# A two-layer decoder trunk on one core: the second layer's input scaled before its split, and places chosen by an assignment

## The chip, the cores and the metric

The kernel runs on one core of one Trainium2 chip, in one launch. The metric is the device time of an execution, in microseconds. Before the change the median of three runs was 2044.93 us (2044.12 to 2046.39).

## The reference

Two layers, each with an input projection that feeds four token mixers, an output projection, and a feed-forward part. All is float32, 1024 tokens by 1024 channels.

```python
for l in range(DEPTH):
    h = rmsnorm(x, attn_norm[l])
    proj = h @ w_in[l]
    (c_q, c_kv, k_r, g_b, g_c, u_conv, u_pool, q_sw, k_sw, v_sw) = jnp.split(proj, pts, axis=-1)
    y_a = mla_attention(c_q, c_kv, k_r, ...)      # latent attention, 4 heads, causal
    y_b = short_gated_conv(g_b, g_c, u_conv, ...) # width 3
    y_c = multiscale_pool(u_pool, ...)            # trailing means over 2, 4, 8, 16
    y_d = swa_sink_attention(q_sw, k_sw, v_sw, ...)  # window 128, sinks
    groups = jnp.stack([y_a, y_b, y_c, y_d], axis=2)  # each normed over its group
    x = x + mixed @ w_o[l]
    h2 = rmsnorm(x, ffn_norm[l])
    gate, up = jnp.split(h2 @ w_gate_up[l], 2, axis=-1)
    x = x + (jax.nn.silu(gate) * up) @ w_down[l]
return rmsnorm(x, final_norm)
```

`rmsnorm(x, g)` is x times the reciprocal root of its mean square ("the root" below) times a gain.

## The kernel before

Activations lie transposed: 128 channels on the partitions, tokens along a row, in tiles of 128x512. There are eight channel blocks d (or k) and two token halves t. Every float32 operand of a product is split in two: a high half in the matmul's own format (a cast on ScalarE, ACT) and a low half, the rest (a subtraction on VectorE, DVE). A product of two such operands is three matmuls, hi·hi, hi·lo, lo·hi (`mm3`, line 281 of the profile). So every weight tile and every activation costs one ACT and one DVE instruction before TensorE (PE) may use it. The feed-forward products are computed block by block with a seven-product scheme, whose sums of weight blocks POOL makes.

The norm ahead of the input projection is not applied to the input. The input x, times its gain, is split at once into `hh[k][t]`. Sums of squares are collected by `SumSq`, and `rnorm` makes the root with a matmul against ones, three ACT operations and two DVE ones; the root of a half stays in `ratt[t]`. Each projection's result in a PSUM bank is multiplied by it as it is taken out (`mul_to(f, p, r_of(t))`, the DVE rows of line 380). At the border of the layers, `done(d, t)` splits a block of the second layer's input as soon as its last down-projection has been added (`evac`, line 1723).

Tiles of SBUF come from 47 pairs of slots (`Slots`, names u), short-lived temporaries from `tmp` (te, tn, tp), results of matmuls from eight PSUM banks (names ps_). All of this is only a first draft of the program. A planner in the same file (`Order`) then traces it, gives each instruction a cost, and looks for an order of the instructions on each engine: a list schedule, then trials that shift ranks and keep what lowers the planned end, averaged over four draws of late loads. It also hands out banks and slots from the planned times, and the program is traced a second time with the order imposed. So what stands where on an engine is the planner's choice, and two programs that differ a little can be ordered quite differently.

PE's main loads in time, from the profile: the first layer's attention part (0 to about 450 us), its feed-forward part (to about 1025), the second layer's attention part (to about 1450), and its feed-forward part with the last norm (to the end).

## Time and profile before

| | before |
|---|---|
| median of three runs | 2044.93 us |
| the profiled execution | 2045.38 us |
| its span, first to last instruction | 2043.6 us |
| PE busy | 2022.9 us, 9398 records |
| DVE busy | 1578.5 us |
| ACT busy | 998.8 us |
| POOL busy | 438.9 us |
| mean granted clock of PE | 0.997 |

In the profile's rows a line number is followed by the engine, the operation, out<-in by the program's names, and the number of instructions. A row of the timeline begins with the start and the duration; what stands in brackets is the idle time of the engine before it and what released it. A line can be that of a helper: line 281 is every three-matmul product, 301 and 304 the high and the low half of a split, 223 and 224 those of a weight tile. PE's ends are modelled, so that a wait shorter than the pipeline's depth does not show as idle.

### The profile page before, as it was taken

The numbers are of one execution on the slowest core, as the hardware profiler recorded it, in microseconds if no ns is written. First come the engines' busy times: TensorE is split into PE (matmuls) and PEld (weight loads), VectorE is DVE, ScalarE is ACT, GpSimd is POOL, SyncE is SP. The second block draws the span as 40 slices with busy tenths as digits, with TensorE's granted clock in tenths as the row PEclk, the third lists the DMA queues.
The fourth block names the chain that finished last, engine by engine and source line by source line (L and its number), as shares of the span: only waits on it lengthen the run. The fifth ranks groups of instructions, "written<-read, shape, count | busy, mean of one in ns | idle before, by whom it ended". The sixth has DMA issues, their size and how long they took to land. (4 is left out here: it accounts for less than half of the span.)

```text
span 2043.6 us, 26485 instructions
## 1 busy us (share of the span) xinstructions
PE 2022.9 (99%) x9398; PEld 1672.6 (82%) x9398; DVE 1578.5 (77%) x2553; ACT 998.8 (49%) x1753; POOL 438.9 (21%) x340
## 2 busy tenths in 40 slices
PE   9999999999999999999999999999999999999998
PEld 7888788878888888888888878888788888888887
DVE  8989979998677777655657999799977777776555
ACT  7458657743333334444434576577433333354342
POOL 0300000025565661000003000000356556500000
PEclk9999999999999999999999999999999999999999
DMA  6310223435555556766513112243455555487542
GB/s 244 127 44 21 84 63 110 149 128 179 179 177 183 176 188 246 259 211 222 176 38 128 56 27 78 65 134 119 145 191 186 177 173 191 169 296 235 195 161 98
DMA packets 144133, 308.13 MB, mean 151 GB/s; under 512 B 14080, under 2 KB 61184, under 8 KB 144000
## 3 DMA queue, kind: packets, MB, share of 16 engines
q1 hardware_dynamic: 144000, 306.43, 44.4%
q8 instruction: 74, 1.21, 0.2%
q14 instruction: 59, 0.48, 0.1%
HBM read 215.67 MB, written 89.65 MB: 149 GB/s over the span
## 5 line engine op out<-in xcount | busy, mean ns | idle before, releaser
L281 PE MATMUL ps_mm<-u,u 128*128 128x512 f32 (+1 forms) x3374 | 843.5, 390 | 7.0 <-ACT u L301 2.8
L281 PEld LDWEIGHTS ps_mm<-u,u 128*128 128x128 f32 x3374 | 615.4, 189 | 129.7 <-ACT u L301 3.6
L281 PE MATMUL ps_s<-u,u 128*128 128x512 f32 x2724 | 652.0, 389 | 0.2 <-DVE u L1214 0.2
L281 PEld LDWEIGHTS ps_s<-u,u 128*128 128x128 f32 x2724 | 510.9, 188 | 108.1 <-DVE u L1214 0.6
L301 ACT CAST u<-u 128x1024 fp32r<-128x1024 f32 (+2 forms) x426 | 361.8, 868 | 478.0 <-PE ps_s L281 116.3
L304 DVE TENSOR_TENSOR u<-u,u 128x1024 fp32r<-128x1024 f32 (+2 forms) x426 | 461.3, 1100 | 154.7 <-ACT u L301 107.0
L281 PE MATMUL ps_t<-u,u 128*128 128x512 f32 (+1 forms) x1092 | 251.9, 377 | 0.0
L281 PEld LDWEIGHTS ps_t<-u,u 128*128 128x128 f32 x1092 | 196.1, 188 | 39.1 <-DVE te L380 0.5
L281 PE MATMUL ps_pv<-u,u 128*128 128x512 f32 x696 | 167.4, 389 | 0.0
L281 PEld LDWEIGHTS ps_pv<-u,u 128*128 128x128 f32 x696 | 130.6, 188 | 27.3 <-DVE tp L1670 0.3
L1277 POOL TENSOR_TENSOR u<-u 128x512 f32<-128x512 f32 x38 | 73.3, 1928 | 226.9 <-DVE u L304 174.2
L1459 ACT ACTIVATE tp<-tp 128x512 f32<-128x512 f32 x76 | 48.0, 632 | 129.3 <-DVE tp L380 129.3
L1062 POOL MEMSET u<- 128x128 f32 x32 | 6.0, 214 | 471.9 <-PE ps_mm L281 250.9
L1247 POOL TENSOR_TENSOR u<-u,u 128x512 f32<-128x512 f32 x38 | 55.6, 1464 | 205.5 <-PE ps_s L281 109.2
L770 POOL TENSOR_TENSOR u<-u,u 128x512 f32<-128x512 f32 x6 | 8.0, 1337 | 413.1 <-ACT sm L628 326.4
L301 ACT CAST u<-ps_t 128x512 fp32r<-128x512 f32 (+3 forms) x132 | 64.8, 502 | 41.3 <-PE ps_t L643 16.6
L1539 POOL TENSOR_TENSOR u<-u 128x352 f32<-128x352 f32 x64 | 79.5, 1244 | 22.4 <-DMA u<-in_w_dn 18.7
L304 DVE TENSOR_TENSOR u<-ps_t,u 128x512 fp32r<-128x512 f32 (+3 forms) x132 | 75.2, 580 | 11.4 <-ACT u L301 10.7
L306 ACT ACTIVATE u<-u,par 128x512 fp32r<-128x512 f32 x92 | 64.6, 719 | 30.7 <-DVE u L380 10.3
L1461 DVE TENSOR_TENSOR tp<-tp,u 128x512 f32<-128x512 f32 x76 | 66.4, 873 | 16.3 <-ACT tp L1459 16.2
L345 ACT ACTIVATE tn<-u 128x512 f32<-128x512 f32 (+1 forms) x91 | 52.6, 597 | 52.2 <-DVE u L1723 45.4
L1249 POOL TENSOR_TENSOR u<-u,u 128x512 f32<-128x512 f32 x38 | 71.8, 1890 | 1.6
(199 smaller groups left out, 2383.5 us busy)
## 6 DMA issues: line engine op xcount, KB each, us to landing
u<-in_w_gu SPq DMA_DIRECT2D x94, 512.0 KB, 4.0
ad<-u SPq DMA_DIRECT2D x154, 256.0 KB, 2.1
u<-ad SPq DMA_DIRECT2D x70, 512.0 KB, 6.0
u<-in_w_dn SPq DMA_DIRECT2D x64, 352.0 KB, 3.3
qd<-u SPq DMA_DIRECT2D x64, 352.0 KB, 2.8
u<-qd SPq DMA_DIRECT2D x32, 512.0 KB, 5.2
u<-in_w_in SPq DMA_DIRECT2D x28, 512.0 KB, 3.9
u<-in_w_dn SPq DMA_DIRECT2D x24, 512.0 KB, 6.5
```

The source lines that it names most:

```text
L281: pe.matmul(o, w, r, start=start and k == 0 and i == 0, stop=stop and k == n - 1 and i == 2, skip_group_check=again,)
L301: a = act.copy(hi, f)
L304: dve.tensor_tensor(out=lo, in0=f, in1=rd(hi), op=ALU.subtract)
L306: a = act.activation(hi, f, AF.Copy, scale=gain)
L345: act.activation(q, f, AF.Square)
L770: pool.tensor_tensor(out=F.ap(q + 1), in0=a21, in1=a22, op=ALU.add)
L1247: pool.tensor_tensor(out=F.ap(q + 1), in0=a21, in1=a22, op=ALU.add)
L1249: pool.tensor_tensor(out=a21, in0=F.ap(q + 1), in1=a11, op=ALU.add)
L1277: pool.tensor_tensor(out=q4, in0=q4, in1=F.ap(self.raw[1] + 1), op=ALU.add)
L1459: last_silu = act.activation(g, g, AF.Silu)
L1461: dve.tensor_tensor(out=g, in0=g, in1=r, op=ALU.mult)
L1539: pool.tensor_tensor(out=o, in0=a, in1=b, op=ALU.add)
```

## The change

Three things are changed.

1. In the second layer, the input is multiplied by gain and root first and split then (`normed`). The projections' results are therefore taken from PSUM unscaled: copied by ACT, split straight from the bank, or multiplied onto another tile. The first layer stays as it is.
2. Slots, PSUM banks and temporaries get their places from one assignment over all tiles (`chains`): the cost of following another tile in its place falls with the time between the two in the plan. The temporaries te, tn and tp share eight places. Before, the place freed last before a tile's start was taken.
3. The planner's search has 40,000 trials in place of 1,500, picks a gap of PE's for each and changes ranks ahead of it, replays only from a stored state, and gives up early where PE's work up to a horizon is not more than before. Its draws make ACT, DVE and POOL late too.

```diff
     def place(self):
-        if self.spans is None:
+        if self.homes is None:
             return self.places.popleft()
-        start, end = self.spans[len(self.made)]
-        i = max(self.places, key=lambda i: u if (u := self.until[i]) <= start else -u)
+        i = self.homes[len(self.made)]
         self.places.remove(i)
-        self.until[i] = end
         return i
...
     def tmp(tag="te"):
-        return tpool.tile([P, HT], F32, name=tag, tag=tag, bufs={"te": 2, "tn": 3, "tp": 3}[tag])
+        if temps is None:
+            t = tpool.tile([P, HT], F32, name=tag, tag=tag, bufs={"te": 2, "tn": 3, "tp": 3}[tag])
+        else:
+            t = tpool.tile([P, HT], F32, name=tag, tag=f"t{next(temp_of)}", bufs=1)
+        slots.temps.append(t.name)
+        return t
...
+        def evict(o, p, t):
+            if l == 0:
+                mul_to(o, p, r_of(t))
+            else:
+                act.copy(o, p)
+        def onto_it(o, p, t):
+            if l == 0:
+                f = tmp()
+                mul_to(f, p, r_of(t))
+                p = f
+            mul_to(o, o, p)
...
         def swa_q(m, pp):
             for t in range(2):
+                e, o = R.half(), R.half()
+                qs[2 * m][t], qs[2 * m + 1][t] = e, o
+                if l:
+                    for h, own, oth in ((e, hd, tl), (o, tl, hd)):
+                        a = R.ap(h)
+                        act.activation(a[own], pp[t][own], AF.Copy, scale=0.125)
+                        dve.scalar_tensor_tensor(
+                            out=a[oth], in0=pp[t][own], scalar=0.125,
+                            in1=rd(a[own]), op0=ALU.mult, op1=ALU.subtract,
+                        )
+                    continue
                 f = tmp()
                 dve.scalar_tensor_tensor(
                     out=f, in0=pp[t], scalar=0.125, in1=r_of(t), op0=ALU.mult, op1=ALU.mult
                 )
...
         for t in range(2):
-            f = tmp()
-            mul_to(f, pk[t], r_of(t))
+            f = pk[t]
+            if l == 0:
+                f = tmp()
+                mul_to(f, pk[t], r_of(t))
             for g, own, oth in ((0, hd, tl), (1, tl, hd)):
...
             f = tmp()
-            mul_to(f, pv_[t], r_of(t))
+            evict(f, pv_[t], t)
...
             tk = rope[t]
-            mul_to(F.ap(tk), F.ap(tk), r_of(t))
+            if l == 0:
+                mul_to(F.ap(tk), F.ap(tk), r_of(t))
...
             a = F.ap(x[d][t])
             if not last:
-                hh[d][t] = half_split(a, pcol(l + 1, PC_ATTN + d))
                 sp.dma_start(xs[d][:, t * HT : (t + 1) * HT], a)
...
-            if not last:
+        def normed(t):
+            r = ss.rnorm(t, tag="pv")
+            for d in range(NK):
+                f = tmp("tp")
+                dve.scalar_tensor_tensor(
+                    out=f, in0=F.ap(x[d][t]), scalar=pcol(l + 1, PC_ATTN + d),
+                    in1=F.ap(r), op0=ALU.mult, op1=ALU.mult,
+                )
+                hh[d][t] = half_split(f)
                 F.free(x[d][t])
+            F.free(r)
...
                 if m == 1:
-                    ratt[0] = ss.rnorm(0, tag="pv")
+                    normed(0)
                 if m == NM - 1:
-                    ratt[1] = ss.rnorm(1, tag="pv")
+                    normed(1)
...
-TRIALS = 1500 if numba else 40
+TRIALS = 40000 if numba else 40
+STOPS, HORIZON = 60, 60.0
...
-        self.lates = np.stack([moves * draw.exponential(0.5, self.n) for _ in range(4)])
+        others = np.array([e in ("Activation", "DVE", "Pool") for e in self.engine])
+        self.lates = np.stack(
+            [
+                draw.exponential(moves * 0.5 + others * 0.03, self.n) - others * 0.03
+                for _ in range(4)
+            ]
+        )
...
+    def chains(start, over, born, gone, places):
+        n = len(start)
+        gap = start[None, :] - over[:, None]
+        cost = np.where(gap > 0, 1.0 / (np.maximum(gap, 0) + 0.5), 10.0 - 10.0 * np.minimum(gap, 0))
+        cost[gone[:, None] >= born[None, :]] = 1e7
+        full = np.zeros((n + places, n + places))
+        full[:n, :n] = cost
+        after = [int(k) for k in linear_sum_assignment(full)[1]]
...
     def banks(self, begin, end):
...
-        for m in tiles:
-            start = min(begin[k] for k in self.users[m])
-            b = max(range(8), key=lambda b: free[b] if free[b] <= start else -free[b])
-            free[b] = max(end[k] for k in self.users[m])
-            given.append(b)
-        return given
+        return self.short(tiles, begin, end, 8)
+    def temps(self, slots, begin, end):
+        return self.short(slots.temps, begin, end, 8)
```

The rest of the diff applies `evict` and `onto_it` at the convolution's and the pooling's projections, takes the latent projections without the product in the second layer, no longer frees `ratt` there, and rewrites the search (`_run`, `_copy`, `_worked`, `_search`) as item 3 says.

Line numbers differ in the two programs: `mm3` is 281 before and 292 after, the root's matmul 361 and 372, a split's low half 304 and 315, a weight tile's low half 224 and 235, a product with the root 380 and 391.

**First place: the first layer's latent queries and the projection behind them (207 us of the profile).** The number at the end of a name is the tile's and is the same in both programs here. VectorE before; tile 2116 is the low half of an input projection's weights, 2122 an eviction of bank ps_mm_2088, line 1007 a row maximum of scores:

```order
L224 TENSOR_TENSOR vlo_2236<-vraw_2233,vhi_2235 128x256
L380 TENSOR_TENSOR u14_503<-u14_503,u29_1991 128x512
L380 TENSOR_TENSOR te_2122<-ps_mm_2088,u4_116 128x512
L380 TENSOR_TENSOR u30_504<-u30_504,u29_1991 128x512
L307 SCALAR_TENSOR_TENSOR u21_2011<-u14_503,par_75,u21_2011 128x512
L1007 ISA ps_s_2133,sm1_2132<-ps_s_2133,cst_76 128x128
L1007 ISA sm1_2132 128x1
L224 TENSOR_TENSOR u14_2116<-u46_2113,u33_2115 128x1024
L380 TENSOR_TENSOR u1_1912<-u1_1912,te_2122 128x512
```

and after (line 1050 is the maximum):

```order
L391 TENSOR_TENSOR te_2119<-ps_mm_2063,u4_116 128x512
L235 TENSOR_TENSOR u3_2116<-u9_2113,u43_2115 128x1024
L318 SCALAR_TENSOR_TENSOR u36_2014<-u34_504,par_75,u36_2014 128x512
L391 TENSOR_TENSOR u5_1912<-u5_1912,te_2119 128x512
L391 TENSOR_TENSOR te_2122<-ps_mm_2088,u4_116 128x512
L1050 ISA ps_s_2133,sm1_2132<-ps_s_2133,cst_76 128x128
L1050 ISA sm1_2132 128x1
```

The low half of the weights stands ahead of the eviction and of the maxima, where it stood behind both. TensorE at the same place; lines 999 to 1001 (1042 to 1044 after) are the scores of one block of queries, ps_mm_2171 and ps_mm_2196 the two token halves of that projection. Before:

```order
L999 MATMUL ps_s_2133<-u0_1846,u43_2060 128x256
L1000 MATMUL ps_s_2133<-u0_1846,u43_2060 128x256
L1001 MATMUL ps_s_2133<-u0_1846,u43_2060 128x256
L281 MATMUL ps_mm_2196<-u22_298,u33_2115 128x512
L281 MATMUL ps_mm_2171<-u15_156,u33_2115 128x512 x2
L281 MATMUL ps_mm_2171<-u15_156,u14_2116 128x512
L281 MATMUL ps_mm_2171<-u16_166,u33_2115 128x512 x2
L999 MATMUL ps_s_2163<-u0_1846,u43_2060 128x512
```

and after:

```order
L1042 MATMUL ps_s_2153<-u23_1846,u35_2060 128x384
L1043 MATMUL ps_s_2153<-u23_1846,u35_2060 128x384
L1044 MATMUL ps_s_2153<-u23_1846,u35_2060 128x384
L1042 MATMUL ps_s_2163<-u23_1846,u35_2060 128x512
L1043 MATMUL ps_s_2163<-u23_1846,u35_2060 128x512
L1044 MATMUL ps_s_2163<-u23_1846,u35_2060 128x512
L292 MATMUL ps_mm_2171<-u15_156,u43_2115 128x512 x2
L292 MATMUL ps_mm_2171<-u15_156,u3_2116 128x512
```

All four score blocks now stand ahead of the projection, which was begun after two of them and cut by the others.

**Second place: ScalarE at the border from attention to feed-forward in the first layer (421 us).** Tile 4420 is the high half of a feed-forward weight sum that matmuls into ps_mm_4436 need; the table load is that of Silu. Before:

```order
L301 CAST u25_4391<-tp_4388 128x512
L301 CAST u44_4395<-tp_4389 128x512
L1459 ACT_TABLE_LOAD
L1459 ACTIVATE u1_4158<-u1_4158 128x512
L301 CAST u5_4420<-u33_4418 128x1024
L301 CAST u31_4405<-tp_4399 128x512
L301 CAST u32_4401<-tp_4398 128x512
```

and after, first the split, then the table load twelve rows on:

```order
L312 CAST u18_4391<-tp_4388 128x512
L1349 COPY u28_4270<-ps_mm_4272 128x512
L312 CAST u1_4420<-u34_4418 128x1024
L312 CAST u25_4381<-tp_4378 128x512
L312 CAST u12_4385<-tp_4379 128x512
L312 CAST u31_4395<-tp_4389 128x512
```

```order
L1363 COPY u7_3845<-ps_mm_4436 128x512
L1363 COPY u9_3998<-ps_mm_4452 128x512
L1503 ACT_TABLE_LOAD
L1503 ACTIVATE u29_4158<-u29_4158 128x512
L1363 COPY u15_4481<-ps_mm_4468 128x512
```

The split was behind the table load and a Silu; it is now ahead of both.

**Third place: the border of the layers, VectorE from the last bank's addition on.** Tile 7423 (before) and 8343 (after) is the sum of squares of t = 1, whose root the chain makes. Names with 9000 and over are the second layer's. Before:

```order
L224 TENSOR_TENSOR u5_9298<-u20_9295,u46_9297 128x1024
L347 SCALAR_TENSOR_TENSOR u15_7423<-tn_8997,u15_7423 128x512
L307 SCALAR_TENSOR_TENSOR u35_8993<-u45_8186,par_75,u35_8993 128x512
L380 TENSOR_TENSOR te_9185<-ps_s_9013,u31_8071 128x512
L304 TENSOR_TENSOR u11_9000<-u15_7423,u11_9000 128x512
L224 TENSOR_TENSOR u6_9452<-u0_9449,u20_9451 128x1024
L562 TENSOR_TENSOR u38_9184<-te_9185,u18_9183 64x512
L563 TENSOR_TENSOR u38_9184<-te_9185,u18_9183 64x512
L562 TENSOR_TENSOR u45_9182<-te_9185,u11_9181 64x512
L563 TENSOR_TENSOR u45_9182<-te_9185,u11_9181 64x512
L373 SCALAR_TENSOR_TENSOR tn_9007<-ps_pv_9003,tn_9007 128x512
L376 SCALAR_TENSOR_TENSOR u15_7423<-tn_9007,tn_9006 128x512
```

and after, behind one more weight split (u25_9324); the tiles tp are the products with gain and root, and what follows alternates a low half and a product to the eighth block:

```order
L358 SCALAR_TENSOR_TENSOR u29_8343<-tn_8990,u29_8343 128x512
L235 TENSOR_TENSOR u18_9478<-u15_9475,u26_9477 128x1024
L315 TENSOR_TENSOR u0_8993<-u29_8343,u0_8993 128x512
L235 TENSOR_TENSOR u12_9644<-u40_9641,u7_9643 128x1024
L235 TENSOR_TENSOR u15_9770<-u2_9767,u41_9769 128x1024
L603 TENSOR_TENSOR u31_9215<-ps_s_9046,u19_9214 64x512
L604 TENSOR_TENSOR u31_9215<-ps_s_9046,u19_9214 64x512
L384 SCALAR_TENSOR_TENSOR tn_9000<-ps_pv_8996,tn_9000 128x512
L387 SCALAR_TENSOR_TENSOR u29_8343<-tn_9000,tn_8999 128x512
L603 TENSOR_TENSOR u39_9217<-ps_s_9046,u32_9216 64x512
L1758 SCALAR_TENSOR_TENSOR tp_9006<-u20_8071,par_75,u29_8343 128x512
L1758 SCALAR_TENSOR_TENSOR tp_9011<-u30_7851,par_75,u29_8343 128x512
```

More weight splits and fewer evictions stand within the chain, and the products come behind it. TensorE there; ps_s_9044 and ps_s_9094 are the values' projection of t = 0 and t = 1, and ps_s_9077, ps_s_9158 and ps_mm_9102 after are the values of t = 0, the queries of t = 0 and the keys of t = 1. Before:

```order
L361 MATMUL ps_pv_9003<-u11_9000,ones_r_79 128x512
L281 MATMUL ps_s_9044<-u26_8463,u41_9041 128x512
L361 MATMUL ps_pv_9003<-u11_9000,ones_r_79 128x512
L281 MATMUL ps_s_9044<-u36_8717,u9_9040 128x512 x2
L281 MATMUL ps_s_9094<-u33_8837,u9_9040 128x512 x2
L281 MATMUL ps_s_9094<-u33_8837,u41_9041 128x512
L281 MATMUL ps_s_9094<-u16_8586,u9_9040 128x512 x2
L281 MATMUL ps_s_9094<-u16_8586,u41_9041 128x512
```

and after:

```order
L292 MATMUL ps_s_9077<-u43_8902,u4_9074 128x512
L292 MATMUL ps_s_9077<-u28_8907,u37_9073 128x512 x2
L292 MATMUL ps_s_9077<-u28_8907,u4_9074 128x512
L292 MATMUL ps_s_9158<-u13_8872,u14_9154 128x512 x2
L292 MATMUL ps_s_9158<-u13_8872,u17_9155 128x512
L292 MATMUL ps_s_9158<-u24_8877,u14_9154 128x512 x2
L292 MATMUL ps_s_9158<-u24_8877,u17_9155 128x512
L292 MATMUL ps_s_9158<-u6_8882,u14_9154 128x512 x2
L292 MATMUL ps_s_9158<-u6_8882,u17_9155 128x512
L292 MATMUL ps_mm_9102<-u35_9008,u38_8808 128x512
L292 MATMUL ps_s_9127<-u35_9008,u37_9073 128x512
```

The second half's first matmul (u33_8837 before, u35_9008 after) came behind the root's matmul by a few rows and did not need the root; now it needs it, and stands after the values and nine matmuls of the queries.

## The prediction

> **What bounds the kernel now.** I read the page's head first, then the windows of the span, the waits of TensorE, and its groups by form in the two attention stretches.

> ```profile
> span 2043.6 us, 26485 instructions
> PE 2022.9 (99%) x9398; PEld 1672.6 (82%) x9398; DVE 1578.5 (77%) x2553; ACT 998.8 (49%) x1753; POOL 438.9 (21%) x340
> ```

> TensorE is the bound: 2022.9 of 2043.6 us. Both programs hold 9384 matmuls of the same kinds and sizes, so the change can only win time in which TensorE waits, or lose some. The profiled execution took 2045.38 us, 1.8 over its span and 0.45 over the median of the three runs (2044.93).

> ```profile
> core 0: us, PE busy (x) PEld busy (x) DVE busy (x) ACT busy (x) POOL busy (x), PEclk, DMA share, GB/s
> 200.00:250.00 50.00, 46.87 (x222) 38.05 (x221) 47.47 (x110) 30.45 (x69) 1.05 (x6) 0.97 0.20 65
> 400.00:450.00 50.00, 48.26 (x205) 38.91 (x203) 48.91 (x74) 30.19 (x50) 4.18 (x3) 0.97 0.25 82
> 500.00:550.00 50.00, 50.00 (x223) 41.39 (x222) 35.36 (x43) 16.15 (x22) 27.70 (x20) 1.00 0.52 176
> 1000.00:1050.00 50.00, 49.96 (x220) 40.70 (x219) 26.31 (x35) 19.39 (x30) 0.00 (x0) 1.00 0.30 105
> 1150.00:1200.00 50.00, 50.00 (x247) 40.87 (x246) 48.19 (x113) 41.62 (x89) 0.00 (x0) 1.00 0.11 33
> 1400.00:1450.00 50.00, 48.67 (x212) 39.23 (x211) 50.00 (x80) 35.10 (x59) 0.00 (x0) 1.00 0.27 85
> 2000.00:2044.00 44.00, 34.41 (x276) 33.36 (x274) 22.92 (x49) 9.39 (x21) 0.00 (x0) 0.94 0.27 96
> ```

> The feed-forward stretches (450 to 1000, 1450 to 2000) have no hole. The holes lie in the attention stretches, where VectorE is busy 47 to 49 of 50 us, and at the end (44.0 - 34.4 = 9.6 us, the last norm's chain, which the change leaves as it is). A busy TensorE hides short waits, because ends are modelled, so I count what the matmuls need. The prices: 512 columns in a row without a hole, then 384, 256 and four transposes by their starts.

> ```profile
> 1818.06 23.12 PE ps_s L281 x102
> 240.41 0.33 PE L1001 MATMUL ps_s<-u,u 128*128 128x384 f32 x1
> 240.58 0.28 PE L999 MATMUL ps_s<-u,u 128*128 128x256 f32 x1
> 240.70 0.28 PE L1000 MATMUL ps_s<-u,u 128*128 128x256 f32 x1
> 1054.31 0.60 PE L570 MATMUL ps_t<-cst,te 128*128 128x128 f32 x4
> 1054.67 4.16 PE L281 MATMUL ps_t<-u,u 128*128 128x512 f32 x17
> ```

> That is 0.2267, 0.17, 0.12 and 0.09 us each. Now the groups by form of 1020 to 1450 (36 rows, the first two and the last), then of 0 to 450 (37 rows, first and last).

> ```profile
> L281 PE MATMUL ps_mm<-u,u 128*128 128x512 f32 x997 | 259.7, 396 | 1.8 <-ACT u L301 1.1 <-DVE u L224 0.6
> L281 PE MATMUL ps_s<-u,u 128*128 128x512 f32 x244 | 60.3, 390 | 0.2 <-DVE u L1214 0.2
> ...
> L1065 PE MATMUL ps_pv<-u 128*128 128x256 f32 x1 | 0.3, 282 | 0.0
> L281 PE MATMUL ps_mm<-u,u 128*128 128x512 f32 x1013 | 271.0, 400 | 5.2 <-DVE u L224 1.9 <-ACT u L301 1.7 <-ACT u L306 1.0
> ...
> L1065 PE MATMUL ps_pv<-u 128*128 128x256 f32 x1 | 0.3, 282 | 0.0
> ```

> By forms, 1020 to 1450 holds 1584 of 512 columns, 40 of 384, 220 of 256, 212 transposes and 8 small: 359.1 + 6.8 + 26.4 + 19.1 + 0.5 = 411.9 us of 430, so 18 us are lost in layer 2. 0 to 450 holds 1619, 40, 220, 212, 8 and the warm-up's 24 (4.6 us): 367.0 + 52.8 + 4.6 = 424.4, so 25.6 us are lost in layer 1. Of the 44 us, this is what shows as waits:

> ```profile
> PE ps_mm L281 <- ACT u L301: 2.8, 2, 1.7
> PE ps_mm L281 <- DVE u L224: 2.5, 2, 1.9
> PE ps_pv L497 <- DVE ones L155: 1.1, 1, 1.1
> PE ps_mm L281 <- ACT u L306: 1.0, 1, 1.0
> PE ps_t L1053 <- DVE u L1037: 0.8, 1, 0.8
> PE ps_s L999 <- ACT u L1018: 0.7, 1, 0.7
> ```

> The third and fourth are the start (2 us) and stay. The first two have one long wait each in layer 1:

> ```profile
> 208.21 1.22 DVE L224 TENSOR_TENSOR u<-u,u 128x1024 fp32r<-128x1024 f32 x1
> 209.49 1.65 PE L281 MATMUL ps_mm<-u,u 128*128 128x512 f32 x3 [1.87 <-DVE u L224]
> 420.04 1.28 ACT L1459 ACT_TABLE_LOAD   x1
> 421.87 1.03 ACT L301 CAST u<-u 128x1024 fp32r<-128x1024 f32 x1
> 422.95 0.74 PE L281 MATMUL ps_mm<-u,u 128*128 128x512 f32 x2 [1.68 <-ACT u L301]
> 424.22 4.14 PE L281 MATMUL ps_mm<-u,u 128*128 128x512 f32 x10
> ```

> At 207 us VectorE splits a weight tile late. At 421 us ScalarE loads a table ahead of a split that TensorE needs. After both, matmuls take 0.41 us in place of 0.23 and the granted clock of the window is 0.97: 3% of 50 us is 1.5 us more. So the two places cost 1.87 + 1.5 and 1.68 + 1.5 = 6.6 us. That leaves 25.6 - 2.0 - 6.6 = 17 us of short waits in layer 1, 18 in layer 2.

> **The change, part by part.** *Unscaled projections in layer 2.* By count of instructions VectorE loses 24 products with a projection's bank, 2 on the rope tables and 4 scaled products of the queries:

> ```profile
> L380 DVE TENSOR_TENSOR te<-ps_mm,u 128x512 f32<-128x512 f32 x19 | 13.1, 687 | 9.9 <-PE ps_mm L281 9.8
> L307 DVE SCALAR_TENSOR_TENSOR u<-u,par,u 128x512 fp32r<-128x512 f32 x30 | 21.8, 745 | 0.0
> ```

> That is 26 x 0.69 + 4 x 0.745 = 20.9 us less on VectorE between 1030 and 1450. The subtractions that now read the bank cost what they did with a temporary (0.69 us with a bank in the first row; 0.69 is also what I take without). ScalarE gets ten plain copies more, some 6 us of an engine that is busy 49%. None of this is TensorE's time; it shortens what TensorE waits for where VectorE is full (48.2 of 50 in 1150 to 1200).

> *The root ahead of the split, at the layers' border.* VectorE gets 16 products (16 x 0.745 = 11.9 us), and its 16 low halves fall from 0.745 to 0.69. It is busy 26.3 of 50 us in 1000 to 1050 and POOL 0.00, so there is room; the question is the chain. For t = 0 the root's matmul now has 66 matmuls behind it (15 us) and nothing waits. For t = 1 the old chain is the measure:

> ```profile
> 1026.01 0.69 DVE L1723 TENSOR_TENSOR u<-u,ps_mm 128x512 f32<-128x512 f32 x1 [5.48 <-PE ps_mm L281]
> 1028.82 0.62 ACT L301 CAST u<-u 128x512 fp32r<-128x512 f32 x1
> 1035.01 0.69 DVE L376 SCALAR_TENSOR_TENSOR u<-tn 128x512 f32<-128x512 f32 x1
> ```

> The last bank's sum begins at 1026.01 and the root is there at 1035.70: 9.7 us. One product and one cast follow (0.75 + 0.62): 11.1. Between the chain's own steps VectorE now has four weight splits (1.22 each) and three subtractions (0.69), 7.0 us; before it had two splits, a scaled half (0.745) and five of 0.69, 6.6 us. So 11.5. TensorE has 59 matmuls without the second half (K and V of t = 0, nine of Q's, two of the sum) before the first that needs it: 59 x 0.2267 = 13.4 us, so the border holds with 1.9 us to spare. Then VectorE makes one operand pair in 0.745 + 0.69 = 1.44 us, and TensorE uses one in six matmuls, 1.36 us, over eight pairs: it trails by 0.6 us. I take +1 us, bounds 0 (the spare holds) and +5 (spare gone, a wait of 3.4 us and a clock dip of 1.5). If the cover is gone, the whole of K and V waits.

> *The order.* 40,000 aimed trials against 1,500, engines' lateness in the draws, and banks, slots and temporaries chosen with room between uses rather than as tight as they fit. What is worth most can be read from the order: the two long waits. At 207 us the low half of the tile (number 2116) now stands ahead of the last eviction (2122) and of all score maxima, and TensorE has four score blocks, twelve matmuls, ahead of the tile's first matmul. At 421 us the split that was behind the table load (4420) stands twelve places ahead of it. Both are two-sided: the waits can go whole (-6.6), or what was held back (Silu, maxima) is late next; I take -5.5. For the short waits no row shows what the search gets. The bounds are 0 and all 35 us. In layer 2, where VectorE also loses 20.9 us, I take a third of 18 (-6); in layer 1, where the same work is only put in another order, a sixth of 17 (-3).

> Sum: -5.5 - 6 - 3 + 1 = -13.5 us: 2045.38 - 13.5 = 2031.9 in the profiled run, 2031.4 by the median; I say 2032.

> [...] The clock is first what the rows say: 0.41 us a matmul right after waits of 1.87 and 1.68 us, and no dip (1.00 in 1400 to 1450) after the other, shorter wait of the first kind (2.8 - 1.7 = 1.1 us), which falls at 1433 us. [...]

> **The rivals.** *Better than that.* With VectorE freed, half of layer 2's 18 us and a third of layer 1's 17 go, and both long waits whole: -6.6 - 9 - 6 + 1 = -20.6, 2024. For it: VectorE is the releaser behind most waits. Against: 20.9 us over eight windows is 2.5 of 50, so it stays above 45 of 50 where it was 48.
> *The search fits the planner's prices, not the chip's.* Long waits go, as many short ones come as leave: -5.5 + 1 = -4.5, 2040. For it: short waits are below what the planner's rounded costs resolve. Against: its draws now have late engines.
> *The dips are not the waits'.* Another cause halves the clock: then 3 us of the 6.6 stay, 2035. Against: both dips stand right behind the two longest waits.
> *Slower: the slots starve the feed-forward.* Every raw tile's place is chosen anew among 47. In 1100 us TensorE waits for nothing there (x223 in 50 us), with DMA at 0.52 and POOL at 27.7 of 50. If a tile's place comes free late in each of the 38 steps of both layers, 0.5 us each is 19 us: -13.5 + 19 = +5.5, 2050. It decides from (13.5 + 4) / 38 = 0.46 us a step. Against: the matmuls of these steps stand in the same blocks of 12 in both orders, and the assignment prefers wide gaps.

> **How the numbers follow.** About 0.2%, 4 us, can be told from no change. Forecast (2027 to 2038): 0.48. Better (2018 to 2027): 0.22. Fits the planner only (2038 to 2045): 0.14, two fifths of it beyond the bound. Dips stay (2033 to 2038): 0.08. Slower: 0.08. Faster 0.48 + 0.22 + 0.06 + 0.08 = 0.84, same 0.08, slower 0.08. The range is 2019 to 2042: it leaves out the end of the better case and the slower one, about 2 in 10 with the tails.

> **What the profile would show.** Right: no window of 50 us with a granted clock under 1.00 before 2000; the list of TensorE's waits without one over 1.5 us; VectorE's busy time lower by some 10 us in all (20.9 + 16 x 0.055 - 11.9), and lower by 20 in 1030 to 1450; TensorE at 49.5 or more in the windows around 1000 to 1050; feed-forward windows at x222 or x223. Wrong: a wait on the split of a product (tile tp) at the border, above 2 us; a feed-forward window with fewer than x221; or attention stretches whose counts by form still leave 40 us over.

## The result, and the profile after

The changed kernel takes 2029.02 us (median; 2028.41 to 2029.48), against 2045.12 us for the kernel before on the same chip: a ratio of 0.9921, 95% interval 0.9904 to 0.9938. That is 16.1 us less; the forecast was 2032, 13 less. The profiled execution took 2029.48 us.

The head of its page:

```profile
span 2027.5 us, 26525 instructions
PE 2013.7 (99%) x9398; PEld 1673.4 (83%) x9398; DVE 1568.0 (77%) x2537; ACT 998.2 (49%) x1763; POOL 446.6 (22%) x340
```

The same windows as before the change (PE, weight loads, DVE, ACT, POOL, then granted clock and DMA):

```profile
core 0: us, PE busy (x) PEld busy (x) DVE busy (x) ACT busy (x) POOL busy (x), PEclk, DMA share, GB/s
200.00:250.00 50.00, 50.00 (x254) 41.88 (x253) 49.81 (x117) 31.96 (x73) 1.05 (x6) 1.00 0.23 76
400.00:450.00 50.00, 50.00 (x222) 41.36 (x221) 50.00 (x69) 27.91 (x44) 11.06 (x7) 1.00 0.40 130
500.00:550.00 50.00, 50.00 (x222) 41.39 (x222) 36.29 (x40) 17.48 (x25) 24.73 (x19) 1.00 0.52 177
1000.00:1050.00 50.00, 49.99 (x222) 40.09 (x221) 42.99 (x62) 27.59 (x46) 5.79 (x4) 1.00 0.33 113
1150.00:1200.00 50.00, 50.00 (x245) 41.48 (x244) 46.69 (x100) 42.04 (x87) 0.00 (x0) 1.00 0.14 40
1400.00:1450.00 50.00, 50.00 (x222) 41.37 (x221) 50.00 (x68) 27.00 (x43) 11.61 (x7) 1.00 0.35 112
```

Both windows of the long waits are full (x254 matmuls for x222, x222 for x205) and their clock is 1.00. In 400 to 450 POOL is busy 11.1 us in place of 4.2: work for the feed-forward part starts earlier. All that TensorE still waits for:

```profile
PE ps_t L684 <- DVE tp L673: 1.1, 2, 0.8
PE ps_pv L536 <- DVE ones L159: 1.1, 1, 1.1
PE ps_s L292 <- DVE te L1702: 1.0, 2, 0.6
PE ps_pv L696 <- DVE u L315: 0.6, 1, 0.6
PE ps_mm L292 <- ACT u L312: 0.6, 1, 0.6
PE ps_s L379 <- ACT tn L378: 0.5, 1, 0.5
```

The longest is 1.1 us and belongs to the start. The groups by form, counted as in the prediction: the two largest of 0 to 450 us (37 rows), then of 1020 to 1450 (36 rows).

```profile
L292 PE MATMUL ps_mm<-u,u 128*128 128x512 f32 x1021 | 264.1, 396 | 0.6 <-ACT u L312 0.6
L292 PE MATMUL ps_s<-u,u 128*128 128x512 f32 x282 | 70.4, 391 | 0.0
```

```profile
L292 PE MATMUL ps_mm<-u,u 128*128 128x512 f32 x989 | 251.5, 395 | 0.0
L292 PE MATMUL ps_s<-u,u 128*128 128x512 f32 x277 | 67.5, 390 | 0.0
```

Summed over the forms of 512 columns, 0 to 450 now holds 1660 matmuls (1619 before) and 1020 to 1450 holds 1619 (1584 before); the smaller forms are equal. At 0.2267 us each, layer 1 has won 41 x 0.2267 = 9.3 us and layer 2 has won 35 x 0.2267 = 7.9 us. Outside these stretches about 1 us was lost again. This count is the yardstick for all experiments below. (The expectations also speak of us lost from start to start, a sum over neighbouring matmuls that puts the two stretches of before at 43 and 33 us, where the forms leave 25.6 and 18. Only differences between kernels are used here.)

### The profile page after: what moved, and what is told of

Read it like the earlier page. It is cut to its first block, busy times and chain, and to the rows that moved or that the text cites. A ratio compares the mean times of both kernels' runs of the same rounds, so it can differ in the third digit from the quotient of the medians.

```text
span 2027.5 us, 26525 instructions
## 1 busy us (share of the span) xinstructions
PE 2013.7 (99%) x9398; PEld 1673.4 (83%) x9398; DVE 1568.0 (77%) x2537; ACT 998.2 (49%) x1763; POOL 446.6 (22%) x340
## 4 chain that ended last, share of the span: by engine, by line
PE 74%; DVE 4%; DMA 1%; issue 0%; POOL 0%; ACT 0%; DVEq 0%; SPq 0%; POOLq 0%
PE ps_s L292 26%; PE ps_mm L292 25%; PE ps_t L292 10%; PE ps_pv L292 8%; DVE u L315 1%; PE ps_pv L1108 1%; PE ps_t L1096 1%; PE ps_s L1043 0%; PE ps_s L1042 0%; PE ps_s L1044 0%; PE ps_s L913 0%; PE ps_t L684 0%; PE ps_s L635 0%; PE ps_pv L696 0%; DVE u L391 0%
## 5 line engine op out<-in xcount | busy, mean ns | idle before, releaser
L292 PE MATMUL ps_mm<-u,u 128*128 128x512 f32 (+1 forms) x3374 | 824.3, 389 | 0.6 <-ACT u L312 0.6
L292 PE MATMUL ps_t<-u,u 128*128 128x512 f32 (+1 forms) x1092 | 247.7, 377 | 0.0
L1320 POOL TENSOR_TENSOR u<-u 128x512 f32<-128x512 f32 x38 | 60.0, 1579 | 225.8 <-DVE u L315 221.1
L1290 POOL TENSOR_TENSOR u<-u,u 128x512 f32<-128x512 f32 x38 | 57.0, 1499 | 218.9 <-DVE u L1371 92.2
L807 POOL TENSOR_TENSOR u<-u,u 128x512 f32<-128x512 f32 x6 | 8.7, 1455 | 375.4 <-DVE u L235 244.2
L1583 POOL TENSOR_TENSOR u<-u 128x352 f32<-128x352 f32 x64 | 84.1, 1314 | 8.2 <-DMA u<-in_w_dn 6.3
L356 ACT ACTIVATE tn<-u 128x512 f32<-128x512 f32 (+1 forms) x91 | 53.5, 598 | 53.9 <-DVE u L1781 48.2
L391 DVE TENSOR_TENSOR tp<-tp,u 128x512 f32<-128x512 f32 x76 | 73.1, 961 | 1.7
L1583 POOL TENSOR_TENSOR u<-u,u 128x352 f32<-128x352 f32 x64 | 73.3, 1145 | 4.3
L1505 DVE TENSOR_TENSOR tp<-tp,u 128x512 f32<-128x512 f32 x76 | 60.8, 800 | 16.0 <-ACT tp L1503 15.4
```

The costliest lines, as they stand in the source:

```text
L292: pe.matmul(o, w, r, start=start and k == 0 and i == 0, stop=stop and k == n - 1 and i == 2, skip_group_check=again,)
L356: act.activation(q, f, AF.Square)
L391: dve.tensor_tensor(out=o, in0=a, in1=b, op=ALU.mult)
L1290: pool.tensor_tensor(out=F.ap(q + 1), in0=a21, in1=a22, op=ALU.add)
L1320: pool.tensor_tensor(out=q4, in0=q4, in1=F.ap(self.raw[1] + 1), op=ALU.add)
L1505: dve.tensor_tensor(out=g, in0=g, in1=r, op=ALU.mult)
```

## The experiments

Times are medians; the ratio is to the kernel before, run beside each on the same chip, with its 95% interval; us "by the ratio" are shares of 2045.1. Beside the runs the kernel before had medians of 2045.1 to 2047.4 us. The last two columns are the matmuls of 512 columns in the two attention stretches, and what their difference from before is worth.

| kernel | us | ratio (95%) | 0 to 450 | 1020 to 1450 |
|---|---|---|---|---|
| before | 2045.1 | 1 | 1619 | 1584 |
| after | 2029.0 | 0.9921 (0.9904 to 0.9938) | 1660, -9.3 us | 1619, -7.9 us |
| e1 planner's half of the change alone | 2028.5 | 0.9915 (0.9901 to 0.9929) | 1662, -9.7 | 1615, -7.0 |
| e2 body alone, planner of before | 2059.7 | 1.0068 (1.0054 to 1.0081) | 1594, +5.7 | 1554, +6.8 |
| e8 the same, another seed | 2055.7 | 1.0049 (1.0038 to 1.0061) | 1612, +1.6 | 1548, +8.2 |
| e3 after, another seed | 2027.9 | 0.9910 (0.9896 to 0.9924) | 1667, -10.9 | 1618, -7.7 |
| e4 after, 1,500 trials | 2028.2 | 0.9913 (0.9899 to 0.9928) | 1662, -9.7 | 1619, -7.9 |
| e7 after, only loads late | 2029.1 | 0.9921 (0.9909 to 0.9933) | 1661, -9.5 | 1619, -7.9 |
| e5 before, new places | 2027.8 | 0.9913 (0.9900 to 0.9926) | 1667, -10.9 | 1614, -6.8 |
| e6 before, new search | 2041.9 | 0.9981 (0.9972 to 0.9989) | 1634, -3.4 | 1591, -1.6 |
| e9 before, new banks | 2039.0 | 0.9967 (0.9954 to 0.9979) | 1650, -7.0 | 1586, -0.5 |
| e10 before, new slots | 2039.6 | 0.9971 (0.9960 to 0.9983) | 1640, -4.8 | 1586, -0.5 |
| e11 before, new places, cost turned round | 2033.2 | 0.9938 (0.9925 to 0.9952) | 1664, -10.2 | 1595, -2.5 |

**e1 and e2: the halves of the change.** e1 is the changed kernel with layer 2 as it was (e2 the reverse: the new layer 2 with the old planner and places):

```diff
         def evict(o, p, t):
-            if l == 0:
-                mul_to(o, p, r_of(t))
-            else:
-                act.copy(o, p)
+            mul_to(o, p, r_of(t))
...
                 if m == 1:
-                    normed(0)
+                    ratt[0] = ss.rnorm(0, tag="pv")
```

> The planner of after (40,000 trials, late engines in the draws, places by the assignment) on the body of before: layer 2's projections are scaled as they leave PSUM, nothing is multiplied by the root ahead of the split. Theory A (two separate gains: the order takes the two long waits of layer 1, 8.6 us in the trace of after; unscaled projections take some 8 us of short waits in layer 2): the planner's half alone, 2045.1 - 8.6 = 2036 us, with layer 1 (0 to 450 us) as in after and layer 2 (1000 to 1450) losing about 33 us as before. Theory B (unscaled projections are what gives all, the order came out better only because the body is lighter): 2042 to 2045, with a long wait still there. Theory C (the search does all, and the freed VectorE is worth nothing): 2029 to 2031, layer 2 losing 25 us.

> Layer 2's input multiplied by its root ahead of the split and its projections unscaled, with the planner of before (1,500 trials, tight places). Theory A: layer 2 loses 25 us in place of 33, layer 1 as a new draw of the old search gives it: 2045.1 - 8 = 2037, and a long wait in layer 1 likely still there. Theory B: 2029 to 2031. Theory C: 2045 or above, VectorE less busy by 10 us and nothing gained. Theory D (the draw of the order alone moves several us either way, whatever is changed): layer 1, whose work is the same as before, differs from before's 43 us of loss by more than 3 us.

e1 took 2028.5 us: the planner's half gives the whole gain, layer 2 included, nearest to theory C. e2 took 2059.7, some 14 us more than before by its ratio; only theory C (2045 or above) leaves room for that, and none named such a loss. Layer 1, where the work is the same as before, lost 5.7 us of it: the draw alone moves that much (theory D). VectorE's busy time did fall, from 1578.5 to 1566.5 us. In e1, which keeps the scaling, the window of 1150 to 1200 reads

```profile
1150.00:1200.00 50.00, 49.95 (x240) 41.09 (x239) 49.15 (x104) 41.57 (x86) 0.00 (x0) 1.00 0.12 32
```

VectorE is at 49.15 of 50 there, 46.69 in the changed kernel, and TensorE is full in both. So the freed VectorE bought nothing that TensorE needed. In e2 the same window is the worst of the trace; first the window, then TensorE's longest waits in e2:

```profile
1150.00:1200.00 50.00, 45.78 (x223) 37.05 (x222) 41.87 (x109) 36.38 (x86) 0.00 (x0) 0.97 0.11 36
```

```profile
PE ps_mm L281 <- ACT u L301: 3.4, 2, 3.0
PE ps_t L673 <- DVE tn L373: 2.6, 1, 2.6
PE ps_t L673 <- DVE u L702: 2.5, 3, 1.6
PE ps_mm L281 <- DVE u L224: 1.9, 1, 1.9
```

VectorE has slack there (41.87) and TensorE still waits for it: ahead of the window attention's transposes (line 673) for line 373, the last step but one of a root. The transposes do not read what that step makes (tn). They read tp, which line 662 wrote last at 1171; what line 373 does with a PSUM bank is read it, and the transposes write one:

```profile
1170.87 0.62 DVE L662 TENSOR_SCALAR tp<-tp,sm 128x256 f32<-128x256 f32 x2
1180.57 0.69 DVE L373 SCALAR_TENSOR_TENSOR tn<-ps_t,tn 128x512 f32<-128x512 f32 x1
1181.32 0.66 PE L673 MATMUL ps_t<-cst,tp 128*128 128x128 f32 x4 [2.62 <-DVE tn L373]
```

So the rows read as a wait for a place: a bank that the root's step has to leave first. The profile does not give the bank's number, so this is a reading and was not tried by itself.

**e8: was e2 a bad draw?** The edit is only the seed.

```diff
-        found = plan.search(trials // 10, r)
+        found = plan.search(trials // 10, r + 20)
...
-    found = plan.search(trials, rounds, rank)
+    found = plan.search(trials, rounds + 20, rank)
```

> The body of after (input multiplied ahead of the split, projections unscaled) under the planner of before, as in the run that took 2059.7 us, with another seed. If those 14 us over before were the luck of one draw of the old search: anything from 2035 to 2060, more than 4 us from 2059.7, with the long waits in other places. If the unscaled body itself is dear under tight places (the root's chain at the border, or the freed VectorE that brings other work together): 2056 to 2063, with the same waits, above all the 10.9 us lost between 1150 and 1200.

2055.7 us, 4.0 less than e2. The same wait, longer still, heads the waits of e8:

```profile
PE ps_t L673 <- DVE tn L373: 4.2, 1, 4.2
```

That lies just outside both ranges. The draw moves several us, but the loss in layer 2 is there in both. Which place makes it was not tried; the rows of e2 above point to a bank. With the new places the same body costs nothing (after against e1: 2029.0 and 2028.5).

**e3, e4, e7: what of the search matters.** Another seed as in e8; the number of trials; and draws that make loads alone late:

```diff
-TRIALS = 40000 if numba else 40
+TRIALS = 1500 if numba else 40
```

```diff
-                draw.exponential(moves * 0.5 + others * 0.03, self.n) - others * 0.03
+                moves * draw.exponential(0.5, self.n)
```

> After with another seed for every search of the planner (seeds 20 higher); the same work. Theory A: within 3 us of after (2026 to 2032), without a long wait, since 40,000 aimed trials remove what the plan shows as a gap. Theory D (the draw decides): more than 4 us from 2029 on either side, and a long wait can be back.

> After with 1,500 trials in place of 40,000; the aimed search, the late engines and the assignment of places stay. If the number of trials is what removes the waits: 2035 to 2040, layer 1 losing 40 us or more as before, layer 2 between. If aiming, late engines and places do it: 2028 to 2032. If every trial gained counts the same: a loss of a few us spread over all attention windows, about 2033.

> After with draws in which the loads alone are late, as before, and the engines keep their planned times. If robustness against late engines is what removes the waits (part of theory S): 2033 to 2040, with a wait over 1.5 us behind VectorE or ScalarE back. Theory P: 2027 to 2031, as after.

2027.9, 2028.2 and 2029.1 us, all within 1.2 us of the changed kernel. With the new places, neither the seed nor the 40,000 trials nor the late engines matter.

**e5 and e6: places or search.** On the kernel before, e5 takes only the assignment (`chains`) for slots, banks and temporaries, e6 only the new search. In e5:

```diff
-        given = plan.banks(begin, end), plan.spans(made, begin, end)
+        given = plan.banks(begin, end), plan.homes(made, begin, end), plan.temps(made, begin, end)
```

> Before with one thing of after: slots, banks and temporaries by the assignment (room between uses, te, tn and tp sharing eight places). Search (1,500 trials, loads alone late in the draws), body and products as in before. The first runs showed that the planner's half alone gives all of the gain (2028.5 us) and that 1,500 trials are enough for it. Theory P (places: a tile in a place that came free just before is bound to the end of the work there, and a slightly late end becomes a wait; wide gaps cut these ties): 2028 to 2032. Theory S (the search, with its aim and its late engines): 2042 to 2047, the attention stretches losing 75 us by start-to-start count as before. Both needed: between, near 2037.

> Before with the other thing of after: the search (40,000 trials aimed at gaps, engines late in the draws), but slots, banks and temporaries by the rule of before (the place that came free last). Theory P: 2042 to 2047, long waits still there. Theory S: 2028 to 2032. Both needed: near 2037.

This settles it: the places alone give 2027.8 us, with the old search and the old layer 2. Nor is it the luck of one draw: the six kernels with the new places lie between 2027.8 and 2029.1 us whatever else they have, the four with the old ones (before, e2, e6, e8) between 2041.9 and 2059.7. The head of e5's page and the windows of the two long waits:

```profile
span 2026.1 us, 26529 instructions
PE 2013.5 (99%) x9398; PEld 1673.8 (83%) x9398; DVE 1580.0 (78%) x2553; ACT 994.7 (49%) x1753; POOL 448.5 (22%) x340
```

```profile
200.00:250.00 50.00, 49.95 (x254) 41.46 (x253) 49.71 (x118) 31.47 (x72) 1.05 (x6) 1.00 0.27 89
400.00:450.00 50.00, 50.00 (x222) 41.32 (x221) 50.00 (x68) 26.91 (x43) 12.12 (x7) 1.00 0.35 117
```

VectorE works as long as before (1580.0 us), and the windows hold what the changed kernel's hold. The search alone gives 3.9 us by its ratio (2.2 to 5.7), no more than another seed moved e2; before itself was not run with another seed. At the two places TensorE now waits 1.17 us (line 380) and 0.78 us; the 1.1 us of the first row fall at 1429 us. The windows are better but not filled (the longest waits, then the windows):

```profile
PE ps_mm L281 <- ACT u L301: 1.8, 2, 1.1
PE ps_mm L281 <- DVE te L380: 1.2, 1, 1.2
```

```profile
200.00:250.00 50.00, 47.88 (x232) 38.81 (x231) 48.91 (x113) 31.97 (x72) 1.05 (x6) 1.00 0.21 69
400.00:450.00 50.00, 48.57 (x210) 38.75 (x209) 50.00 (x72) 29.83 (x48) 8.30 (x5) 1.00 0.31 101
```

**e9, e10, e11: which places, and is it the room?** On the kernel before: banks alone, slots alone, and all places with the cost turned round, so that a tile follows the one that came free shortest before it.

```diff
-        cost = np.where(gap > 0, 1.0 / (np.maximum(gap, 0) + 0.5), 10.0 - 10.0 * np.minimum(gap, 0))
+        cost = np.where(gap > 0, np.minimum(gap, 1000.0) * 1e-3, 10.0 - 10.0 * np.minimum(gap, 0))
```

> Before with the PSUM banks alone by the assignment; slots by the rule of before, te, tn and tp in their own buffers, search as before. All three together in the old search gave 2027.8 us. If banks are the tie (VectorE and ScalarE wait for TensorE's last reader of a bank): 2028 to 2034. If slots are (the trace of before has VectorE waiting 4.8 us at 105 us for TensorE before it may split a weight tile into a slot): 2042 to 2047. If each gives a part: near 2037, and banks and slots add to the whole or fall short by what the temporaries give.

> Before with the 47 pairs of slots alone by the assignment; banks by the rule of before, te, tn and tp in their own buffers, search as before. If slots are the tie: 2028 to 2034, and VectorE's wait of 4.8 us at 105 us is gone. If banks are: 2042 to 2047. If each gives a part: near 2037.

> Before with all places by the assignment, as in the run that took 2027.8 us, but with the cost turned round: a tile follows in its place the one that came free shortest before it, as in the old rule. If room between uses is what counts: 2040 to 2050. If it is the assignment itself (one solution over all tiles, no tile placed before its place is free in the plan) or the shared temporaries: 2028 to 2032.

Banks alone give 6.8 us by their ratio, slots alone 5.9; of the 17.8 of e5 5.1 are left for the temporaries or for having them together, which was not told apart. VectorE's wait of 4.8 us at 105 us that an expectation names is gone in e10, but also in e9, where the slots go by the old rule; it was no sign of the slots. With the cost turned round 12.7 us of the 17.8 stay, between the two forecasts. So some 70% come from one solution over all tiles (or from the shared temporaries), and 5 us from room between uses. Each of these three is one draw, and with the old places a seed moved 4 us: that banks, slots and room each give a part is likely, their sizes are rough. In layer 1 tight or wide does not matter (-10.2 and -10.9 us); it does in layer 2 (-2.5 and -6.8).

**e12: the price of a dip.** A program of its own: groups of matmuls, ahead of each a chain of VectorE products that TensorE waits for, with a growing number of matmuls meant to cover the chain.

```python
for i in range(n):                       # n = 60 - late
    pe.matmul(a, w[:, c : c + P], first if i == 0 else x, ...)
for i in range(late):                    # meant to run while the chain runs
    pe.matmul(b, w[:, c : c + P], x, ...)
```

> Another program: it computes nothing of the reference and writes a part of x to the output. Three times 17 groups of 60 matmuls of 512 columns; ahead of each group TensorE waits for a chain of six VectorE products (some 4.4 us), which starts ever earlier before the group's end, so that the wait shrinks from about 4.5 us to about 0.8 us in steps of 0.23. It prices a clock dip by the length of the wait. If a wait of 1.7 to 1.9 us is enough to halve the clock, as the two places of before suggest: matmuls spaced by 0.41 to 0.45 us for about 3.4 us after every wait above some 1.7 us, none after shorter ones. [...] If the position of the wait against a fixed period counts: dips after some waits of one length and not after others, over a band of lengths.

The sweep failed: the covering matmuls were put elsewhere. They cover the first 20 chains whole, and of the 30 waits left 29 came out at the full length, 4.4 us, and the first at 2.60. It answers only for long ones. The windows ahead of the waits and with them, the waits in all, and two rows of the timeline:

```profile
0.00:360.00 360.00, 351.97 (x1526) 285.79 (x1526) 87.16 (x126) 2.85 (x3) 0.20 (x4) 1.00 0.04 14
360.00:909.00 549.00, 415.86 (x1534) 328.43 (x1534) 124.72 (x181) 0.00 (x0) 0.00 (x0) 0.86 0.00 0
```

```profile
PE pa L84 <- DVE y L97: 130.7, 30, 4.4
```

```profile
379.14 0.80 PE L84 MATMUL pa<-y,wr 128*128 128x512 f32 x1 [4.42 <-DVE y L97]
379.73 14.61 PE L84 MATMUL pa<-x,wr 128*128 128x512 f32 x54
```

Without waits the clock is 1.00, with a wait of 4.4 us every 18 us it is 0.86. Over the 549 us that is 0.14 x 549 = 77 us lost, some 2.6 us for each of the 30 waits; a dip of before lost 1.7 (last section).

No kernel beats the changed one beyond the intervals: e5 and e3 are 1.2 us below it, with intervals that overlap.

## Why the prediction was right, and where its reasons were wrong

**The bound held.** VectorE's busy time, layer 2's instructions and the search could each be put back, and only what filled TensorE's holes moved the time. (The rows hold 9398 matmuls in both programs, where the prediction says 9384; no sum uses it.) The count by forms turns into the measured time throughout: in e5 10.9 + 6.8 = 17.7 us for 17.8 by the ratio, in e2 5.7 + 6.8 = 12.5 us lost for some 14.

**The two long waits (-5.5 taken, -6.6 as bound).** Both are gone, whole. A dip was priced a little low: in before it is 3.41 us at a clock of 0.50, 1.7 us lost and not 1.5 (last section), so the bound is 7.0. With the short ones (-3 taken) layer 1 was to win 8.5 us and won 9.3. The order showed it rightly, but the step named the wrong agent in part: the search alone (e6) leaves waits of 1.17 and 0.78 us there and the windows at x232 and x210; the places alone (e5) fill them.

**Layer 2 (-6 taken, +1 at the border).** It won 7.9 us, and the step that failed is its reason. I took a third of 18 us because "VectorE also loses 20.9 us" there. e1 wins 7.0 us in layer 2 with none of that; the unscaled projections are worth at most the 0.9 us between 1615 and 1619 matmuls, of which the whole time shows nothing (2029.0 us for 2028.5). The stretch was not short of VectorE's time: it was short of freedom to place the work. That reading (an instruction that writes a place must wait for its last reader, and no order can move it ahead of that) is argued, with e2's wait for line 373 as one case; that the places decide is shown.

**The border (+1, bounds 0 and +5).** As forecast. TensorE shows 49.99 of 50 in 1000 to 1050, and the root's products, tiles tp, hold weight loads up only a little (groups of tile tp between 1000 and 1060, then who waited for them):

```profile
L1758 DVE SCALAR_TENSOR_TENSOR tp<-u,par,u x16: 739/744/1774, 1002.6 to 1035.0; 128x512 f32<-128x512 f32 x16
...
  PEld ps_mm L292: 1.6, 6
```

A product takes 0.744 us (0.745 taken). e1, without them, has x226 matmuls in that window for x222, some 0.9 us.

**VectorE's busy time.** 1578.5 - 1568.0 = 10.5 us less in all, "some 10" forecast. "Lower by 20 in 1030 to 1450" missed:

```profile
1030.00:1450.00 420.00, 416.21 (x2020) 341.41 (x2019) 363.48 (x776) 254.85 (x542) 19.50 (x28) 1.00 0.24 81
```

```profile
1030.00:1450.00 420.00, 419.55 (x2057) 349.83 (x2056) 353.78 (x761) 256.99 (x553) 26.70 (x31) 1.00 0.25 84
```

The first row is before, the second after: 9.7 us. A fixed window holds other work once the program runs ahead (x2057 matmuls for x2020), and the border's last products (up to 1035.0) lie in it; how much each takes was not counted. That forecast should have been made on groups, not on times.

**The rivals.** *Better than that* (2024) came no nearer than 2027.8. *The search fits the planner's prices* (2040): the search alone (e6) did give 2041.9, so for the search this rival was right; I had put the places and the search into one term, "the order", and asked only what trials get. *Slots starve the feed-forward* (2050): no; 500 to 550 holds x222 matmuls, and the only trace of it is two waits, 1.0 us together, on a sum of that part (te, line 1702), which before does not have. *The dips are not the waits'* (2035): in after, with no wait over 1.1 us, the clock is 1.00 from 6.49 to 2020.35 us, and in e6, with waits of 1.2 us and less at those places, it is 1.00 there. In the timelines of before, after and e4 to e11 between 40 and 2000 us, all three waits of 1.96 us or more (1.96 in e10, 2.20 in e9, 4.22 in e8) are followed by halved matmuls, three of six between 1.65 and 1.95 are (with the 1.95 of e2), and none under that. Two places tell it: rows of the timeline of e9 and its window, then a row of e2, whose window of 200 to 250 has a clock of 1.00.

```profile
1424.53 0.50 PE L282 MATMUL ps_s<-u,u 128*128 128x512 f32 x1 [2.20 <-ACT u L302]
1426.00 4.30 PE L282 MATMUL ps_mm<-u,u 128*128 128x512 f32 x11 [0.26 <-ACT u L302]
```

```profile
1400.00:1450.00 50.00, 47.54 (x201) 38.29 (x201) 48.35 (x71) 30.90 (x50) 5.15 (x3) 0.97 0.22 69
```

```profile
212.67 0.96 PE L281 MATMUL ps_mm<-u,u 128*128 128x512 f32 x3 [1.95 <-DVE u L224]
```

In e9 eleven matmuls take 4.30 us, where at 0.2267 a start and 0.39 for the last they would take 2.66; in e2, after 1.95 us, three take 0.96, where they would take 0.84.

**What was luck.** The bound, 44 us of holes, was right, but the shares taken of it (a sixth of the short waits in layer 1, a third in layer 2) had no row behind them. That the sum, -13.5, came near the measured -16.1 rests on these guesses, and the one for layer 2 had the wrong reason. The share that the change got, 17.2 of 44, could not have been read from the trace of before.

## What to carry to other kernels

When instructions are ordered by a planner, look at what the places (slots, banks, temporaries) forbid before giving the planner more trials or the engines less work: here the places alone gave all of the gain, more search alone 4 us (what a seed can move), and less work on the second busiest engine nothing. Price holes by counting matmuls by form in a stretch and comparing with another kernel's count in the same stretch; it gave every result here within some 2 us. An engine that is 96% busy beside the bound (48.19 of 50 us) is not yet the reason for the bound's waits; put its work back and see.

## What the runs showed of the hardware

In before the granted clock is 0.50 from 209.30 to 212.71 us, from 424.34 to 427.75 and, in the last norm, from 2038.84 on. The first begins 0.19 us ahead of the end of its wait (209.49), the second 1.39 us behind it (422.95). Each of the two lasts 3.41 us, and at half rate that is a loss of 1.7 us on top of the wait: the ten matmuls from 424.22 take 4.14 us, where at 0.2267 a start and 0.39 for the last they would take 2.43. After e8's wait of 4.22 us the loss is larger: 31 matmuls from 1179.16 take 9.86 us, where they would take 7.19.

What differs between waits of the same length shows in narrow windows. The three stretches of before begin 215.04 and 1614.50 us apart, 63 and 473 times 3.413 us. Before's wait of 1.68 us lies whole in the 3.41 us ahead of the second stretch. In e8 the halved matmuls behind the wait of 1.87 us begin at some 211.8 us (41 from 211.77 take 11.09 us, where they would take 9.46). Counted on from there in steps of 3.413 us, the 263rd ends at 1109.49, within the wait of 1.77 us that ends at 1109.97. The step with the wait and the next one, first before, then e8:

```profile
420.93:424.34 3.41, 1.67 (x7) 0.80 (x6) 3.41 (x6) 3.40 (x6) 0.00 (x0) 1.00 0.06 17
424.34:427.75 3.41, 3.41 (x9) 2.63 (x10) 3.41 (x7) 1.68 (x3) 0.00 (x0) 0.50 0.40 137
```

```profile
1106.08:1109.49 3.41, 2.12 (x10) 1.42 (x8) 3.38 (x4) 0.96 (x2) 1.93 (x2) 1.00 0.73 281
1109.49:1112.90 3.41, 2.93 (x16) 2.52 (x17) 3.09 (x5) 1.69 (x3) 0.00 (x0) 1.00 0.09 31
```

TensorE is idle for 1.74 us of before's step, and the clock of the next is 0.50; it is also idle for 1.82 us of the 3.41 ahead of the first stretch (205.89 to 209.30). In e8 it is idle for 1.29 and 0.48 us, and the clock stays at 1.00. This speaks for the idle time within one step, and not the length of the wait, as what counts; that is a reading of these three places, and no run varied the one without the other. Why the loss after e8's wait of 4.22 us is larger was not worked out.
